# A list scheduler's cost figures set to other values, and PSUM evictions given another claim on buffers

## The chip, the cores and the metric

One NeuronCore of a Trainium2 chip. The metric is the device time of one execution in microseconds (us), the median of several runs. The time of one profiled execution stands beside it.

## The reference

Two layers of a decoder trunk with 512 tokens, 16 learned meta tokens ahead of them (528 columns) and a width of 2048. Everything is float32. Cut to what matters, one layer is:

```python
proj = h @ w_in                                   # 2048 -> 5120
c_val, c_glu, c_gate, q, k, v, a_gate, r_x, r_gate = split(proj)
c = depthwise_conv31(c_val * sigmoid(c_glu))
c = silu(layer_norm(c)) @ conv_pw_w + conv_pw_b
y_conv = c * silu(c_gate)
q, k = partial_rotary(q), partial_rotary(k)
y_attn = sliding_window_sink_attention(q, k, v) * silu(a_gate)
r = depthwise_conv4(r_x)
y_lru = rg_lru(r) * silu(r_gate)                  # a gated linear recurrence over positions
h = layer_norm(ALPHA * h + concat(y_conv, y_attn, y_lru) @ w_out)
```

A layer norm stands ahead of the first layer; the meta tokens are dropped from the output.

## The kernel before

Activations lie transposed: 128 channels on the partitions and the 528 tokens along a row, so the 2048 channels are 16 tiles. A float32 product is made of three float32r products (`mm3`): the rounded weight with the rounded activation, the rounded weight with the activation's remainder, and the weight's remainder with the rounded activation. Every weight block therefore comes by DMA into one of two raw buffers (`w`), ScalarE (ACT) rounds it and VectorE (DVE) subtracts to get the remainder (`weight_split`); the activations are split in the same way (`split`, and in `turn` and `normal` for the layers' inputs). The input projection of a layer has 40 column tiles, the output projection 16, each a sum over 16 row tiles. A full column tile is 96 products of 264 columns; where the second layer leaves the meta tokens out, a tile is 48 products of 512 columns.

No order is written out by hand. Each piece of work (`glu`, `val`, `rope`, `recur`, `gate`, `conv_taps`, `normal` and so on) is a generator that yields operations, allocations and conditions, a thread with a priority (a smaller number goes first). The class `Sched` runs these threads when the program is built: `run` looks at the head operation of each thread, works out when it could start (`_start`: when its engine is free by the costs booked so far, and when its operands are there by the hand-off times in `LAT`), and emits the operation with the earliest believed start; priority breaks ties. Each engine gets its instructions in the order in which they were emitted and carries them out in that order on the chip. So the booked costs decide nothing but the order. They are in `V` (DVE), `S` (ACT), `mm` and `tr` (TensorE, PE) and `dma` (the queue that SyncE issues).

Buffers come from pools: 78 activation rows (`u`), two PSUM tiles of two banks (`p`), four single banks (`b`), four temporaries (`t`), and others. An ordinary request for a `u` row is granted only while more than `10 - 2 * wheld` rows are free, `wheld` being the weight blocks split and not yet used up (`_head`); requests for split weights take the last row. A product's PSUM tile comes free after the thread that takes it has copied it out.

What the steps below touch: the statistics of the first two token tiles and their normalization (`x_norm`, `x_turn`, `turn`) with the first three column tiles (`gemms`); the end of layer 1 (`gather`, `square`, `norm`, `normal`), where the column sums of `norm` go through PE, a RECIPROCAL on DVE gives the scale of one half of the tokens, and each of 16 `normal` threads makes one tile of layer 2's input, the last step of which is a subtraction on DVE (the tile's remainder); and the recurrence (`recur`), of which at most two run at once and which has 12 products of its own.

Of the kernel before, what the change touches and what calls it, by code (L numbers as in the profile page):

```python
# [9 lines left out]
F32 = mybir.dt.float32  # L10
# [8 lines left out]
L = SEQ + NM  # L19
# [48 lines left out]
FULL = [(0, 0, HALF), (1, HALF, HALF)]  # L68
# [14 lines left out]


class Alloc:
    def __init__(self, kinds, dt=F32, w=L, weight=False):
        self.kinds, self.dt, self.w, self.weight = kinds, dt, w, weight


class Until:  # L90
# [4 lines left out]
class Sched:  # L95
# [5 lines left out]
    def __init__(self, tc, nc, pools):  # L101
        self.tc, self.nc, self.pools = tc, nc, pools
        self.free = dict.fromkeys("TVSGQ", 0.0)
        self.free["Q"] = 0.8
        self.fixed = ()
        self.threads = []
        self.written, self.read = {}, {}
        self.slots = {k: [(0.0, "Q", i) for i in range(n)] for k, (p, shape, n) in pools.items()}
        self.where = {}
        self.serial = 0  # L110
        self.wheld = self.steps = self.table = 0
# [65 lines left out]

    def mm(self, out, w, x, start, stop):
        n = self._size(x)
        c = max(n / 2400, self._size(w) / 1200) + 0.003  # L180
        if w.dtype == F32:
            c = 4 * c + 0.23
        f = self.nc.tensor.matmul
        return self._op("T", c, [out], [w, x], lambda: f(out, w, x, start=start, stop=stop))  # L184
# [5 lines left out]
    def dma(self, out, in_):  # L190
        f = self.nc.sync.dma_start
        n = 4 * self._size(out) * out.shape[0]
        o, i = ([a] if a.tensor.name in self.where or a.tensor.name in self.fixed else [] for a in (out, in_))
        return self._op("Q", max(0.45, n / 360e3), o, i, lambda: f(out=out, in_=in_), 2.0)  # L194


    def spawn(self, prio, gen):
# [12 lines left out]
    def _head(self, th):  # L210
        while True:
            r = th[3]
            if r is None or isinstance(r, Op):
                return r
            if isinstance(r, Event):
                if not r.done:
                    return None
                self._step(th, None)
            elif isinstance(r, Until):
                if not r.test():  # L220
                    return None
                self._step(th, None)
            else:
                kind = next((c for c in r.kinds if len(self.slots[c]) > (0 if r.weight or c != "u" else max(0, 10 - 2 * self.wheld))), None)
                if kind is None:
                    return None
                self._step(th, self.alloc(kind, r.dt, r.w))
# [45 lines left out]
def body(tc, nc, ctx, t):  # L273
# [85 lines left out]

    def U(dt=F32, w=L):  # L360
        return Alloc("u", dt, w)


    class Weight:
# [188 lines left out]
        pass  # L553

    def glu(y, j, pr):
        e = yield U()
        if j == 0:
            y.turn = yield Alloc("a")
        for pv, ev in pr.views(e):
            yield S(out=ev, in_=pv, func=AF.Tanh, scale=0.5)  # L560
        pr.free()
        y.glu[j] = e

    def val(y, j, pr):
        c = yield U()
        yield Until(lambda: y.glu[j] is not None)
        e = y.glu[j]
        for (pv, ev), (_, cv) in zip(pr.views(e), pr.views(c)):
            yield V("scalar_tensor_tensor", out=cv, in0=ev, scalar=1.0, in1=pv, op0=ALU.add, op1=ALU.mult)
        pr.free()  # L570
        k.release(e)
        k.spawn(6, conv_taps(y, j, c))
# [62 lines left out]
        k.release(y.turn)  # L635

    def conv_point(y, j, pr):
        o = yield U()
        for pv, ov in pr.views(o):
            yield S(out=ov, in_=pv, func=AF.Identity, scale=0.5, bias=P(y.l, "pb", j))  # L640
        pr.free()
        y.branch[8 + j] = o

    def rope(pr):
        a = pr.a
        x = yield U()
        s = yield U()
        for pv, xv in pr.views(x):
            yield S(out=xv, in_=pv, func=AF.Copy)
        pr.free()  # L650
        yield V("stream_shuffle", out=s[:, a:L], in_=x[:, a:L], mask=list(range(8, 16)) + list(range(8)) + list(range(16, 32)))
        yield V("tensor_tensor", out=x[:, a:L], in0=x[:, a:L], in1=cos[:, a:L], op=ALU.mult)
        yield V("tensor_tensor", out=s[:, a:L], in0=s[:, a:L], in1=sin[:, a:L], op=ALU.mult)
        yield V("tensor_tensor", out=x[:, a:L], in0=x[:, a:L], in1=s[:, a:L], op=ALU.add)
        k.release(s)
        return x
# [25 lines left out]
        k.release(x)  # L682

    def values(y, p, pr):
        x = yield U()
        m = yield U()
        for pv, xv in pr.views(x):
            yield S(out=xv, in_=pv, func=AF.Copy)
        pr.free()
        mv = m[:, 0:384].rearrange("p (n c) -> p n c", n=3)  # L690
        yield S(out=mv[:, :, 0:16], in_=x[:, 0:16].unsqueeze(1).to_broadcast([128, 3, 16]), func=AF.Copy)
        for i in range(3):
            yield S(out=mv[:, i, 16:128], in_=x[:, 88 + 100 * i:200 + 100 * i], func=AF.Copy)
        ps = []
        for _ in range(2):
            b = yield Alloc("b")
            ps.append(b)
        for n, pieces in enumerate(VCHUNKS):
            src = x[:, pieces[0][0]:pieces[0][0] + 128] if len(pieces) == 1 else mv[:, n // 2 - 1, :]
            yield k.tr(ps[n // 4][:, 128 * (n % 4):128 * (n % 4) + 128], src, ident)  # L700
        out = []
        for n in range(0, 8, 2):
            v = yield U(F32R, 512)
            v4 = v.rearrange("p (c g s d) -> p c g s d", c=2, g=2, s=2)
            p4 = ps[n // 4][:, 128 * (n % 4):128 * (n % 4) + 256].rearrange("p (c g d) -> p c g d", c=2, g=2)
            yield S(out=v4[:, :, :, 0, :], in_=p4, func=AF.Copy)
            yield V("tensor_tensor", out=v4[:, :, :, 1, :], in0=p4, in1=v4[:, :, :, 0, :].bitcast(F32), op=ALU.subtract)
            out.append(v)
        k.release(*ps, x, m)
        y.values[p] = out  # L710
# [107 lines left out]
            k.release(w)  # L818
            y.rw.append(p)

    def recur(y, j, pr):

        l, d = y.l, dp[y.l]
        x = yield U()
        for pv, xv in pr.views(x):
            yield S(out=xv, in_=pv, func=AF.Copy)
        pr.free()
        yield Until(lambda: y.busy < 2)
        y.busy += 1
        y.rgo = True  # L830
        r = yield U()
        yield S(out=r, in_=x, func=AF.Identity, scale=P(l, "lw", 12 + j), bias=P(l, "lb", j))
        for i in (2, 1, 0):
            s = 3 - i
# [32 lines left out]
    def gate(y, j, pr):  # L867

        a = pr.a
        e = yield U()  # L870
        for pv, ev in pr.views(e):
            yield S(out=ev, in_=pv, func=AF.Tanh, scale=0.5)
            yield V("scalar_tensor_tensor", out=ev, in0=ev, scalar=1.0, in1=pv, op0=ALU.add, op1=ALU.mult)
# [14 lines left out]
    def project(y, x, ready, phases):  # L888
# [12 lines left out]

        def step(fn, i, rngs, xs=x):
            pr = yield from gemm(xs, rngs)
            k.spawn(2 if fn is not recur else 7, fn(y, i, pr))

        k.spawn(0.2, recur_weights(y))
        todo = [(val, 1, FULL)][group - 3:]
# [1 line left out]
            todo += [(glu, j, FULL), (val, j, FULL)]  # L909
        todo += [(keys, 0, FULL), (values, 0, FULL)]  # L910
        todo += [(queries, j, rq) for j in range(4)]
        todo += [(recur, j, FULL) for j in range(4)]
        todo += [(keys, 1, FULL), (values, 1, FULL)]
        todo += [(gate, j, rq) for j in range(4)]
        todo += [(conv_point, j, rq, y.cx) for j in range(4)]
# [372 lines left out]
```

## Time and profile before

| | us |
|---|---|
| runs of the kernel | 1490.9, 1490.77, 1488.93 (median 1490.77) |
| the profiled execution | 1489.76 |
| its span | 1488.0 |
| PE busy in the span | 1451.8 (98%) |
| DVE busy | 1049.1 (71%) |
| ACT busy | 706.3 (47%) |

The mean granted clock of TensorE over the span was 0.995 of full speed. Times in rows are counted from the start of the span. A matmul's record is longer than the distance to the next one, since products are pipelined; so a stream of them is read by its starts or by a long row of the chain, and an idle time by the gap that a row names together with the lengths of the records around it.

### The profile page before, as it was taken

How to read it: one execution, taken by the hardware profiler on the slowest of the kernel's cores; microseconds unless marked ns; L12 is line 12 of the kernel's file. 1: busy time of each engine (PE TensorE's matmuls, PEld its weight loads, DVE VectorE, ACT ScalarE, POOL GpSimd, SP SyncE). 2: the span in 40 equal slices, each digit the busy share in tenths (PEclk: the TensorE clock that was granted, in tenths of full speed). 3: DMA queues.
4: the chain of work that ended last, by engine and by line, in shares of the span. 5: the costliest groups of instructions: out<-in, count | busy, mean ns of one | idle time of the engine just before them, and what ended most of it. 6: DMA issues, size and time to landing. Idle time of an engine off the chain costs nothing.

```text
span 1488.0 us, 25171 instructions
## 1 busy us (share of the span) xinstructions
PE 1451.8 (98%) x10028; PEld 1350.8 (91%) x10028; DVE 1049.1 (71%) x2111; ACT 706.3 (47%) x1539; POOL 20.3 (1%) x28
## 2 busy tenths in 40 slices
PE   4999999999999999999999999999999999999996
PEld 3999999999999999999999997998788888888885
DVE  7798999984588443354688889999747864434437
ACT  5412458883377332222368134778735853323221
POOL 2200000000000000000000000000000000000000
PEclk9999999999999999999999999999999999999999
DMA  6312522243221223232433033223232222523323
GB/s 231 93 57 85 143 86 65 62 138 106 80 72 58 85 86 114 72 100 85 132 111 93 29 107 120 79 61 118 88 103 86 71 72 90 163 88 114 100 71 113
DMA packets 56549, 142.32 MB, mean 96 GB/s; under 512 B 12464, under 2 KB 20912, under 8 KB 56432
## 3 DMA queue, kind: packets, MB, share of 16 engines
q1 hardware_dynamic: 56432, 140.73, 30.8%
q8 instruction: 78, 1.28, 0.4%
q14 instruction: 39, 0.32, 0.1%
HBM read 128.12 MB, written 4.19 MB: 89 GB/s over the span
## 4 chain that ended last, share of the span: by engine, by line
PE 88%; DVE 7%; ACT 2%; DMA 1%; issue 1%; SPq 0%; DVEq 0%; ACTq 0%
PE p L184 68%; PE b L184 18%; DVE u L160 5%; PE b L188 2%; DVE a L160 2%; ACT u L174 1%; DMA w<-in_win 1%; DVE s L160 0%; DMA a<-in_x 0%; DVE t L160 0%; ACT t L174 0%; DVE P L160 0%; DMA u<-u 0%; SPq L194 0%; PE p L188 0%
## 5 line engine op out<-in xcount | busy, mean ns | idle before, releaser
L184 PE MATMUL p<-u,u 128*128 128x264 f32 (+3 forms) x7824 | 1181.4, 306 | 4.1 <-DVE u L160 2.9
L184 PEld LDWEIGHTS p<-u,u 128*128 128x128 f32 x7824 | 1064.5, 189 | 61.8 <-DVE u L160 4.6
L160 DVE TENSOR_TENSOR u<-w,u 128x512 fp32r<-128x512 f32 x456 | 306.0, 689 | 174.0 <-ACT u L174 170.6
L174 ACT ACTIVATE u<-w 128x512 fp32r<-128x512 f32 x456 | 273.0, 622 | 241.8 <-DMA w<-in_wout 124.3
L184 PE MATMUL b<-u,u 128*128 128x512 f32 (+6 forms) x1568 | 290.5, 324 | 4.3 <-DVE u L160 3.2
L184 PEld LDWEIGHTS b<-u,u 128*128 128x128 f32 (+2 forms) x1568 | 241.4, 185 | 33.9 <-DVE u L160 4.6
L160 DVE SCALAR_TENSOR_TENSOR a<-u,dp,a 128x527 f32<-128x527 f32 (+14 forms) x240 | 179.7, 749 | 4.2
L174 ACT ACTIVATE P<-P,s 100x257 f32<-100x257 f32 (+5 forms) x240 | 111.2, 479 | 28.7 <-DVE s L160 28.7
L160 DVE TENSOR_TENSOR u<-u,u 128x528 f32<-128x528 f32 (+5 forms) x146 | 100.8, 697 | 20.8 <-ACT u L174 17.9
L174 ACT ACTIVATE u<-p 128x528 f32<-128x528 f32 (+2 forms) x71 | 42.4, 598 | 149.0 <-PE p L184 148.8
L174 ACT ACTIVATE u<-u 64x528 fp32r<-64x528 f32 (+5 forms) x112 | 63.8, 584 | 81.0 <-DVE u L160 74.9
L160 DVE SCALAR_TENSOR_TENSOR u<-u,p 128x528 f32<-128x528 f32 (+3 forms) x45 | 30.7, 683 | 68.7 <-ACT u L174 50.6
L174 ACT ACTIVATE t<-b 128x400 fp32r<-128x400 f32 (+3 forms) x112 | 57.1, 510 | 44.0 <-PE b L184 22.0
L160 DVE CUSTOM_DVE_ANT_0 P<-b,con,nsink 100x256 f32<-100x256 f32 (+2 forms) x160 | 67.1, 450 | 3.1 <-PE b L184 2.2
L160 DVE TENSOR_TENSOR t<-b,t 128x400 fp32r<-128x400 f32 (+2 forms) x72 | 41.7, 579 | 13.4 <-ACT t L174 13.0
L184 PE MATMUL b<-t,u 128*128 128x400 f32 (+2 forms) x144 | 50.5, 351 | 0.0
L188 PE MATMUL b<-con,P 100*128 100x100 f32 (+2 forms) x320 | 44.1, 253 | 0.0
L174 ACT ACTIVATE u<-b 128x256 fp32r<-128x256 f32 (+4 forms) x28 | 11.8, 443 | 57.7 <-PE b L188 51.1
L188 PEld LDWEIGHTS b<-con,P 100*128 100x128 f32 (+2 forms) x320 | 35.9, 140 | 3.1 <-DVE s L160 0.4
L160 DVE TENSOR_SCALAR P<-P,s 100x256 f32<-100x256 f32 (+3 forms) x88 | 31.5, 363 | 0.7
L160 DVE SCALAR_TENSOR_TENSOR u<-u,u 128x528 f32<-128x528 f32 (+1 forms) x40 | 27.5, 699 | 5.2 <-ACT u L174 4.7
L174 ACT ACTIVATION_READ_ACCUMULATOR P<-P,s 100x1 f32 (+2 forms) x160 | 30.2, 189 | 0.0
(103 smaller groups left out, 656.7 us busy)
## 6 DMA issues: line engine op xcount, KB each, us to landing
w<-in_win SPq DMA_DIRECT2D x160, 512.0 KB, 3.7
w<-in_wout SPq DMA_DIRECT2D x64, 512.0 KB, 4.1
u<-u SPq DMA_DIRECT2D x48, 120.0 KB, 2.2
a<-in_x SPq DMA_DIRECT2D x8, 256.0 KB, 5.1
P<-in_x SPq DMA_DIRECT2D x8, 256.0 KB, 6.0
u<-u SPq DMA_DIRECT2D x16, 128.0 KB, 2.1
w<-in_pw SPq DMA_DIRECT2D x8, 256.0 KB, 2.6
out<-a SPq DMA_DIRECT2D x8, 256.0 KB, 2.3
```

What stands on the lines that cost most here:

```text
L160: return self._op("V", c, outs, ins, lambda: f(**kw))
L174: op = self._op("S", c, outs, ins, lambda: f(**kw))
L184: return self._op("T", c, [out], [w, x], lambda: f(out, w, x, start=start, stop=stop))
L188: return self._op("T", max(2 * self._size(ident) / 2400, 0.11) + 0.005, [out], [x, ident], lambda: f(out, x, ident))
```

## The change

The booked durations change in three places. A product of n columns was booked at n/2400 us or the weight's columns/1200, whichever is more, and 0.003; it is now 0.000445 n or the same second term, and 0.0045. That is 0.113 before and 0.122 now for 264 columns, 0.216 and 0.232 for 512. A DMA was booked at its bytes/360,000 us and landed 2.0 later; now it is bytes/400,000 and 2.65, which for 512 KB is 3.46 before and 3.96 now. The queue is believed free from 0.75 on, before 0.8.

The row into which a PSUM tile is copied is now asked for with `E()`, which is granted while more than `4 - 2 * wheld` rows are free, in `glu`, `val`, `conv_point`, `rope`, `values` and `gate`. The second row of `rope` and `values` is asked for only after the PSUM tile has been given back. In the recurrence the copy out of PSUM becomes a thread of its own, `take_rx`, with `E()` and priority 2, which then starts `recur` at priority 7; before, the copy was the first step of `recur` and had priority 7.

```diff
-    def __init__(self, kinds, dt=F32, w=L, weight=False):
+    def __init__(self, kinds, dt=F32, w=L, weight=False, keep=10):
...
-        self.free["Q"] = 0.8
+        self.free["Q"] = 0.75
...
-        c = max(n / 2400, self._size(w) / 1200) + 0.003
+        c = max(0.445e-3 * n, self._size(w) / 1200) + 0.0045
...
-        return self._op("Q", max(0.45, n / 360e3), o, i, lambda: f(out=out, in_=in_), 2.0)
+        return self._op("Q", max(0.45, n / 400e3), o, i, lambda: f(out=out, in_=in_), 2.65)
...
-                kind = next((c for c in r.kinds if len(self.slots[c]) > (0 if r.weight or c != "u" else max(0, 10 - 2 * self.wheld))), None)
+                kind = next((c for c in r.kinds if len(self.slots[c]) > (0 if r.weight or c != "u" else max(0, r.keep - 2 * self.wheld))), None)
...
+    def E(keep=4):
+        return Alloc("u", F32, L, False, keep)
...
     def rope(pr):
         a = pr.a
-        x = yield U()
-        s = yield U()
+        x = yield E()
         for pv, xv in pr.views(x):
             yield S(out=xv, in_=pv, func=AF.Copy)
         pr.free()
+        s = yield U()
...
-    def recur(y, j, pr):
-
-        l, d = y.l, dp[y.l]
-        x = yield U()
+    def take_rx(y, j, pr):
+        x = yield E()
         for pv, xv in pr.views(x):
             yield S(out=xv, in_=pv, func=AF.Copy)
         pr.free()
+        k.spawn(7, recur(y, j, x))
+
+    def recur(y, j, x):
+
+        l, d = y.l, dp[y.l]
...
-            k.spawn(2 if fn is not recur else 7, fn(y, i, pr))
+            k.spawn(2, fn(y, i, pr))
...
-        todo += [(recur, j, FULL) for j in range(4)]
+        todo += [(take_rx, j, FULL) for j in range(4)]
```

The other five threads replace `U()` by `E()` in the same way. No operation is added or dropped: both programs have 10,022 matmuls and transposes on PE, 1,927 scheduled operations on DVE, 1,364 on ACT, 24 on GpSimd (POOL) and 395 DMAs. What changes is their order on each engine and the buffers that they get. In the pieces of that order below, a name is its pool, the count of the allocation and the tile's number; the last 200 operations of PE stand alike in both.

At the start, on DVE. `a_33` is the first token tile and `a_39` the second, BN_AGGR closes the statistics of the first. Before:

```order
L160 BN_STATS s_40_132<-a_33_121 128x6 x4
L160 BN_AGGR s_41_133<-s_40_132 128x2
L160 BN_STATS s_42_142<-a_39_131 128x6
L160 RECIPROCAL s_41_133<-s_41_133 128x1
L160 BN_STATS s_42_142<-a_39_131 128x6
L160 SCALAR_TENSOR_TENSOR s_41_133<-s_41_133 128x1
```

Now:

```order
L160 BN_STATS s_40_132<-a_33_121 128x6 x4
L160 BN_STATS s_42_140<-a_39_131 128x6
L160 BN_AGGR s_41_133<-s_40_132 128x2
L160 BN_STATS s_42_140<-a_39_131 128x6
L160 RECIPROCAL s_41_133<-s_41_133 128x1
L160 BN_STATS s_42_140<-a_39_131 128x6
L160 SCALAR_TENSOR_TENSOR s_41_133<-s_41_133 128x1
```

The first chunk of the second tile now has its statistics taken ahead of the first tile's BN_AGGR.

A little later on DVE, before the first weight of the third column tile gets its remainder (`u_86` before, `u_83` now, 128x512), which the third column tile's products on PE wait for. Before:

```order
L160 BN_STATS s_71_217<-P_57_185 128x6
L160 CAST u_15_101<-t_91_284 128x256
L160 TENSOR_SCALAR P_44_152<-P_44_152,s_52_177 128x512
L160 TENSOR_TENSOR u_16_102<-t_91_284,u_15_101 128x256
L160 CAST u_17_103<-t_93_294 128x256
L160 CAST u_19_105<-t_95_300 128x256
L160 TENSOR_SCALAR P_45_153<-P_45_153,s_52_177 128x512
L160 TENSOR_TENSOR u_86_263<-w_59_191,u_85_262 128x512
```

Now:

```order
L160 BN_STATS s_63_200<-P_54_177 128x6
L160 CAST u_13_99<-t_89_276 128x256
L160 TENSOR_SCALAR P_44_148<-P_44_148,s_52_173 128x512
L160 CAST u_15_101<-t_91_285 128x256
L160 CAST u_17_103<-t_93_292 128x256
L160 TENSOR_TENSOR u_16_102<-t_91_285,u_15_101 128x256
L160 TENSOR_TENSOR u_83_245<-w_65_204,u_82_244 128x512
```

The remainder stands ahead of one CAST and of the second normalized chunk (`P_45`), and one BN_STATS (of the fourth tile) has also gone behind it.

At the end of layer 1, on DVE. `a_1062` holds the scale of the tokens; its first write is a row of `norm` for the first half, which reads PSUM (`b`), and the 128x512 rows are remainders of weights. Before:

```order
L160 TENSOR_TENSOR a_1059_7223<-a_1059_7223,u_1258_9075 128x264
L160 TENSOR_TENSOR a_1059_7223<-a_1059_7223 128x264
L160 TENSOR_TENSOR u_1263_9112<-w_1252_9021,u_1262_9111 128x512
L160 TENSOR_TENSOR a_1062_7231<-b_1266_9128,a_1062_7231 128x264
L160 TENSOR_TENSOR u_1268_9137<-w_1257_9069,u_1267_9136 128x512
L160 TENSOR_TENSOR u_1270_9153<-w_1257_9069,u_1269_9152 128x512
L160 SCALAR_TENSOR_TENSOR u_1238_8930<-u_1238_8930,b_1259_9076 128x264
L160 TENSOR_TENSOR u_1238_8930<-u_1238_8930,a_1059_7223 128x264
L160 RECIPROCAL a_1062_7231<-a_1062_7231 128x264
```

Now:

```order
L160 TENSOR_TENSOR a_1059_7223<-a_1059_7223,u_1258_9076 128x264
L160 TENSOR_TENSOR u_1261_9095<-w_1252_9010,u_1260_9094 128x512
L160 TENSOR_TENSOR a_1059_7223<-a_1059_7223 128x264
L160 TENSOR_TENSOR a_1062_7231<-b_1263_9113,a_1062_7231 128x264
L160 TENSOR_TENSOR u_1265_9118<-w_1252_9010,u_1264_9117 128x512
L160 TENSOR_TENSOR u_1268_9137<-w_1257_9065,u_1267_9136 128x512
L160 RECIPROCAL a_1062_7231<-a_1062_7231 128x264
L160 TENSOR_TENSOR u_1270_9155<-w_1257_9065,u_1269_9154 128x512
```

The row of `norm` stands right behind the last addition of squares (`a_1059`), with no weight's remainder between, and its RECIPROCAL two places earlier. On PE the two products of `norm` stand ten places earlier.

The same place, some 45 rows on: the second half of the tokens. The rows that read a `t` write a remainder of layer 2's input, in the order of its tiles. Before:

```order
L160 TENSOR_TENSOR u_1313_9388<-t_1314_9389,u_1312_9387 128x264
L160 TENSOR_TENSOR P_1147_8096<-P_1147_8096,a_1062_7231 128x264
L160 TENSOR_TENSOR P_1159_8220<-P_1159_8220,a_1062_7231 128x264
L160 TENSOR_TENSOR u_1316_9393<-t_1317_9394,u_1315_9392 128x264
L160 RECIPROCAL a_1062_7231<-a_1062_7231 128x264
L160 TENSOR_TENSOR u_1319_9423<-t_1320_9424,u_1318_9422 128x264
L160 TENSOR_TENSOR a_1062_7231<-b_1307_9369,a_1062_7231 128x264
```

Now:

```order
L160 TENSOR_TENSOR u_1316_9398<-t_1317_9399,u_1315_9397 128x264
L160 TENSOR_TENSOR P_1159_8220<-P_1159_8220,a_1062_7231 128x264
L160 TENSOR_TENSOR u_1171_8344<-u_1171_8344,a_1062_7231 128x264
L160 TENSOR_TENSOR u_1319_9403<-t_1320_9404,u_1318_9402 128x264
L160 RECIPROCAL a_1062_7231<-a_1062_7231 128x264
L160 TENSOR_TENSOR u_1322_9431<-t_1323_9432,u_1321_9430 128x264
L160 TENSOR_TENSOR a_1062_7231<-b_1312_9381,a_1062_7231 128x264
```

The RECIPROCAL stands behind `u_1319`, which is tile 6 here, where before it stood behind `u_1316`, tile 5.

In layer 2, on PE, around the first gate tile (`p_1815` before, `p_1814` now; 128x512). The 128x264 products into `b` are those of the fourth recurrence. Before:

```order
L184 MATMUL p_1773_12588<-u_1345_9576,u_1766_12544 128x512
L184 MATMUL p_1773_12588<-u_1346_9577,u_1766_12544 128x512
L184 MATMUL p_1773_12588<-u_1345_9576,u_1767_12545 128x512
L184 MATMUL b_1813_12771<-u_1807_12751,u_1575_11447 128x264
L184 MATMUL b_1813_12771<-u_1808_12752,u_1575_11447 128x264
L184 MATMUL b_1813_12771<-u_1807_12751,u_1576_11448 128x264
L184 MATMUL p_1815_12781<-u_1286_9258,u_1769_12581 128x512
L184 MATMUL p_1815_12781<-u_1287_9259,u_1769_12581 128x512
L184 MATMUL p_1815_12781<-u_1286_9258,u_1770_12582 128x512
L184 MATMUL b_1816_12789<-u_1807_12751,u_1575_11447 128x264
L184 MATMUL b_1816_12789<-u_1808_12752,u_1575_11447 128x264
L184 MATMUL b_1816_12789<-u_1807_12751,u_1576_11448 128x264
```

Now:

```order
L184 MATMUL p_1814_12788<-u_1304_9345,u_1775_12616 128x512
L184 MATMUL p_1814_12788<-u_1305_9346,u_1775_12616 128x512
L184 MATMUL p_1814_12788<-u_1304_9345,u_1776_12617 128x512
L184 MATMUL p_1814_12788<-u_1307_9356,u_1782_12648 128x512
L184 MATMUL p_1814_12788<-u_1308_9357,u_1782_12648 128x512
L184 MATMUL p_1814_12788<-u_1307_9356,u_1783_12649 128x512
L184 MATMUL p_1814_12788<-u_1315_9397,u_1782_12648 128x512
L184 MATMUL p_1814_12788<-u_1316_9398,u_1782_12648 128x512
L184 MATMUL p_1814_12788<-u_1315_9397,u_1783_12649 128x512
L184 MATMUL b_1818_12822<-u_1807_12762,u_1575_11449 128x264
L184 MATMUL p_1814_12788<-u_1318_9402,u_1782_12648 128x512
```

Before, all twelve products of the recurrence stood among the first products of this gate tile, the first three of them ahead of it; now eighteen of the gate's products stand ahead of the first of the recurrence's, and they are spread out behind.

## Rows read from the trace of the kernel before

**Rows 1.** The page: busy time by engine, and the chain's shares.

```profile
PE 1451.8 (98%) x10028; PEld 1350.8 (91%) x10028; DVE 1049.1 (71%) x2111; ACT 706.3 (47%) x1539; POOL 20.3 (1%) x28
...
PE 88%; DVE 7%; ACT 2%; DMA 1%; issue 1%; SPq 0%; DVEq 0%; ACTq 0%
```

**Rows 2.** Stretches: length, busy per engine (x instructions), granted clock, DMA share, GB/s.

```profile
20.00:30.00 10.00, 6.97 (x31) 4.84 (x30) 10.00 (x22) 6.34 (x14) 6.83 (x8) 0.85 0.23 71
30.00:40.00 10.00, 10.00 (x73) 10.00 (x72) 9.14 (x22) 4.70 (x9) 2.84 (x3) 0.81 0.72 226
40.00:1477.00 1437.00, 1431.21 (x9918) 1333.72 (x9917) 1010.08 (x2027) 683.90 (x1498) 9.73 (x12) 1.00 0.30 92
80.00:160.00 80.00, 80.00 (x661) 80.00 (x660) 72.83 (x118) 19.16 (x35) 0.00 (x0) 1.00 0.25 75
740.00:800.00 60.00, 58.86 (x470) 57.76 (x469) 54.53 (x132) 43.99 (x85) 0.00 (x0) 1.00 0.28 83
800.00:900.00 100.00, 100.00 (x770) 97.30 (x770) 85.31 (x133) 33.87 (x63) 0.00 (x0) 1.00 0.32 97
900.00:1050.00 150.00, 147.03 (x1024) 136.30 (x1023) 143.19 (x316) 108.53 (x263) 0.00 (x0) 1.00 0.29 90
```

**Rows 3.** The chain that ended last: start, length, what (x instructions).

```profile
489.55 239.90 PE p L184 x1966
...
1214.24 77.73 PE p L184 x336
```

**Rows 4.** Timeline of the start: start, length, engine, instruction [idle before <-what ended it].

```profile
6.95 0.26 DVE L160 BATCH_NORM_AGGREGATE s<-s 128x2 f32<-128x24 f32 x1
...
8.73 0.69 DVE L160 BATCH_NORM_STATS2 s<-a 128x6 f32<-128x512 f32 x1 [1.51 <-DMA a<-in_x]
...
10.17 1.52 ACT L174 ACTIVATE a<-a,s 128x512 f32<-128x512 f32 x2 [2.62 <-DVE s L160]
...
25.81 0.48 DVE L160 CAST u<-t 128x256 fp32r<-128x256 f32 x2
...
26.21 0.97 DVE L160 TENSOR_SCALAR P<-P,s 128x512 f32<-128x512 f32 x1
...
27.10 1.21 DVE L160 TENSOR_TENSOR u<-w,u 128x512 fp32r<-128x512 f32 x1
...
28.37 0.58 PE L184 MATMUL b<-u,u 128*128 128x256 f32 x1 [2.04 <-DVE u L160]
```

**Rows 5.** Timeline at the end of layer 1, DVE and PE.

```profile
774.06 1.80 DVE L160 RECIPROCAL a<-a 128x264 f32<-128x264 f32 x1 [0.40 <-ACT a L174]
...
775.78 0.37 DVE L160 TENSOR_TENSOR u<-t,u 128x264 fp32r<-128x264 f32 x1
...
777.64 0.28 PE L184 MATMUL p<-u,u 128*128 128x264 f32 x1
...
778.12 0.42 DVE L160 TENSOR_TENSOR u<-t,u 128x264 fp32r<-128x264 f32 x1
...
778.60 0.88 PE L184 MATMUL p<-u,u 128*128 128x264 f32 x5 [0.68 <-DVE u L160]
```

**Rows 6.** Timeline, four late starts of PE elsewhere.

```profile
75.33 0.75 PE L184 MATMUL p<-u,u 128*128 128x264 f32 x4 [0.21 <-ACT u L174]
...
290.85 0.63 PE L184 MATMUL p<-u,onesr 128*128 128x264 f32 x3 [0.64 <-DVE u L160]
...
1028.64 1.43 PE L184 MATMUL p<-u,u 128*128 128x512 f32 x5 [0.70 <-ACT u L174]
...
1045.67 0.50 PE L184 MATMUL p<-u,u 128*128 128x512 f32 x1 [0.69 <-DVE u L160]
```

**Rows 7.** The page's DMA groups (KB, us to landing); a group of DVE (busy, mean).

```profile
w<-in_win SPq DMA_DIRECT2D x160, 512.0 KB, 3.7
...
w<-in_wout SPq DMA_DIRECT2D x64, 512.0 KB, 4.1
...
L160 DVE TENSOR_TENSOR_SCAN u<-u,u 128x528 f32<-128x528 f32 x8 | 9.9, 1246 | 0.0
```

More of the change, by code (lines that the diff above doesn't have):

```diff
@@ L85 @@
 class Alloc:
-    def __init__(self, kinds, dt=F32, w=L, weight=False):
-        self.kinds, self.dt, self.w, self.weight = kinds, dt, w, weight
+    def __init__(self, kinds, dt=F32, w=L, weight=False, keep=10):
+        self.kinds, self.dt, self.w, self.weight, self.keep = kinds, dt, w, weight, keep
 class Until:
@@ L555, in glu @@
     def glu(y, j, pr):
-        e = yield U()
+        e = yield E()
         if j == 0:
@@ L564, in val @@
     def val(y, j, pr):
-        c = yield U()
+        c = yield E()
         yield Until(lambda: y.glu[j] is not None)
@@ L637, in conv_point @@
     def conv_point(y, j, pr):
-        o = yield U()
+        o = yield E()
         for pv, ov in pr.views(o):
@@ L684, in values @@
     def values(y, p, pr):
-        x = yield U()
-        m = yield U()
+        x = yield E()
         for pv, xv in pr.views(x):
@@ L689, in values @@
         pr.free()
+        m = yield U()
         mv = m[:, 0:384].rearrange("p (n c) -> p n c", n=3)
@@ L819, in recur_weights @@
             y.rw.append(p)
-    def recur(y, j, pr):
-        l, d = y.l, dp[y.l]
-        x = yield U()
+    def take_rx(y, j, pr):
+        x = yield E()
         for pv, xv in pr.views(x):
@@ L869, in gate @@
         a = pr.a
-        e = yield U()
+        e = yield E()
         for pv, ev in pr.views(e):
```

## The prediction, made before the changed kernel ran

> **What bounds the kernel now.** Read the page's busy times first, then the chain, then PE's idle time by stretches. PE works 1451.8 of 1488 us, and the chain that ended last lies on it for 88% [rows 1]. Neither number tells what PE's pace is; the chain's long rows do. 1966 products of 264 columns take 239.90 us, so 122.0 ns each, and 336 of 512 columns take 77.73, so 231.3 ns each [rows 3]. No operand is late there. This work is the same after the change, product for product, so some 1,450 us can't move; only PE's late starts can, and the start and the tail, which are fixed by other engines.
>
> How much are the late starts? From 40 to 1477 us PE is busy 1431.21 of 1437, so it shows 5.8 us of idle time [rows 2]. That is too little: the record of one 264-column product is 0.28 us long [rows 5], 0.16 more than the pace, so each late start hides another 0.16. The timeline has 16 of them, the first at 75.33 and the last at 1045.67 [rows 6]; 16 times 0.16 is 2.6, and the whole is 8.4 us. By place: the end of layer 1 (740 to 800) 1.14 idle and six starts, 2.1; layer 2's attention and recurrence (900 to 1050) 2.97 and five, 3.8 [rows 2]; the other five 1.7 and 0.8, so 2.5. Their releasers are mostly DVE. [...]
>
> **The change, part by part.** None of it alters an operation, so the price of each edit is what the new order does at those places.
>
> *The booked product.* 0.113 and 0.216 become 0.122 and 0.232, which is what rows 3 measure. With the old figures the scheduler believed PE 7% faster than it is; it put PE's next products, and the work that feeds them, ahead of whatever DVE could have done meanwhile. With the new ones DVE is believed to have more room and takes more of the convolution's taps before the same product of PE: some 8 to 15 more by the time the scores of either layer begin. The room is there: DVE works 72.83 of 80 us in 80 to 160 and 85.31 of 100 in 800 to 900, while PE doesn't idle in either [rows 2]. Each tap that moves forward leaves later DVE time free where DVE is nearly full, 143.19 of 150 in 900 to 1050 [rows 2]. That is the gain's main source.
>
> [...]
>
> *The booked DMA.* For 512 KB the landing moves from 3.46 to 3.96 us; the medians are 3.7 and 4.1 [rows 7]. It only moves requests earlier or work on a weight later. Weights are split some 90 products (11 us) ahead of PE in both orders, and PE's late starts name ACT or DVE, not a DMA [rows 6]: taken at nothing in the steady part. At the start it moves a row: below.
>
> *Evictions with `E()`, and `take_rx`.* A copy out of PSUM may now take a row when more than 4 are free, and the recurrence's copy no longer has the lowest claim. PE waited at 1028.64 for such a copy, 0.70 idle and 0.16 hidden [rows 6]. If rows run out elsewhere instead, an ordinary request waits; cover for that is DVE's and ACT's idle time, and without it the price is one late start, 0.4 to 0.9 each as in rows 6.
>
> *The start.* The first tile's BN_AGGR now stands behind a statistic that waits for its DMA until 8.73; it ran at 6.95 [rows 4]. So it ends at about 9.7 instead of 7.2, and the first normalization on ACT begins at about 11.1 instead of 10.17 [rows 4]. DVE does not lose all of this: 1.51 us it waited for that DMA anyway, and it has other statistics to do; it loses the 0.26 of BN_AGGR, which no longer fills the wait, and some 0.2 behind the root on ACT, 0.5 in all. Against that, the remainder of the third weight has less ahead of it: a statistic (0.69), a normalized chunk (0.97) and a CAST (0.24) [rows 4], 1.9 us. DVE has no gap there, so the remainder ends 1.4 earlier than 28.31 (27.10 and 1.21), and PE, which took it up at 28.37 [rows 4], goes on at about 27.0. I take 1.3 off. Bounds: if PE is soon short of normalized inputs, which are moved back by the same rows, nothing is kept and the 0.9 of the later first normalization is lost; if the clock comes back earlier too, up to 2.5 is won.
>
> *The end of layer 1.* The row of `norm` stands ahead of a weight's remainder (some 0.7, as the 128x512 row in rows 4 at 8.73) and its products ten places earlier on PE (1.2 us), so the scale of both halves is there about 1.2 earlier. PE's last late start there is tile 7's remainder: it came behind a RECIPROCAL of 1.80 and tile 6's, and PE started at 778.60 instead of 777.76 (777.64 and the pace), 0.84 late [rows 5], on top of a smaller lateness for tile 6. With the RECIPROCAL one tile later, tile 6's goes; with everything 1.2 earlier most of tile 7's is covered too. Of 2.1 I leave 0.6: minus 1.5.
>
> *Layer 2, 900 to 1050.* The two starts at 1044 and 1045.67 come from a recurrence whose products stand in fours with single gate products, so that a DVE remainder is waited for with nothing else to do. With eighteen gate products (4.2 us by rows 3) ahead, both have cover. The copy at 1028.64 is moved up by its claim. Of 3.8 I leave 1.3: minus 2.5.
>
> *The other five.* The scores' first product and the means of the convolution's norm (290.85, 0.64 idle [rows 6]) are chains of DVE and ACT that taps moved forward shorten but don't remove: of 2.5 I leave 1.5, minus 1.0.
>
> *New waits.* In the new order an operand's last step stands five to seven products ahead of its use, 0.6 to 0.85 us, and one subtraction of 264 columns takes 0.42 [rows 5] besides hand-offs: it holds, but thinly. For eight new late starts of 0.16 I add 1.3.
>
> Sum: -1.3 - 1.5 - 2.5 - 1.0 + 1.3 = -5.0. Against the profiled execution's 1489.76 that is 1484.8. That execution lies 1.0 under the runs' median of 1490.77, so for the median I say **1485.8**.
>
> **The rivals.**
> *The waits only move (no difference).* PE's work is fixed, and DVE's too; with a truer table the scheduler spends the cover that the false one left by mistake. If each wait that goes comes back as another of like size, 3 to 4 us of the 6.3 won are lost, and the time is 1488 to 1491. For it: the thin lead above. Against: the places that wait now are where DVE is full, and taps do go out of them.
> *DVE is over-filled (slower).* The old table's 7% made PE really arrive later than believed, a cover for everything DVE is booked too cheaply for. The recurrence's scan is booked at 0.615 (its 528 columns and 62, by 960 MHz) and takes 1.246 [rows 7]; eight of them are 5.0 us short, and they lie where DVE is at 143.19 of 150. If the taps that fill 60 to 180 and 800 to 900 also stand ahead of remainders that PE now reaches on time, PE waits for the 5.0, none of the old 6.3 in layers goes, and the time is 1490.8 + 5.0 - 1.3 = 1494.5. It decides from the point at which DVE has no gap left before a remainder: 85.31 of 100 and some ten taps more (7 to 8 us) is 93, under it. So it is less likely than the forecast.
> *More is won.* All 8.4 us go and the start gives 2.5: 1479.9. It needs the scores' and means' chains to vanish, which no moved row does.
> *The order doesn't do what the change says.* The moved rows stand in the order as told, so only their effect is open; no chance of its own.
>
> **How the numbers follow.** A measurement of this kernel can tell about 0.2%, 3.0 us, from no change: faster is under 1487.8, slower over 1493.8. The forecast (most waits go, 1482 to 1487.8) has 0.56; more is won (under 1482) 0.08; the waits only move (1487.8 to 1493.8) 0.25; over-filled DVE, or the start's loss together with it, 0.11. So faster 0.64, same 0.25, slower 0.11. The range leaves out most of the greater gain (0.06), the slower case (0.11) and the upper end of the middle one (0.03): 1481.5 to 1491.5.
>
> **What would show it right or wrong.** Right: PE goes on at about 27.0 at the start; the stretch around the end of layer 1 has under 0.5 of visible idle time and the attention and recurrence of layer 2 under 1.2; DVE is over 90 of 100 busy in 800 to 900; the pace of the long rows stays at 122 and 231 ns. Wrong: PE resumes after 28.4 or the granted clock stays low past 34; new gaps in 60 to 160 or 800 to 900 released by DVE, which is the over-filled case; or gaps released by ACT, where a row (`u`) was missing.

## The result: 20 us slower, and the profile after

The changed kernel takes 1510.23 us (1507.62 to 1511.55) where the kernel before, run beside it, takes 1490.03. The ratio is 1.0132 with an interval of 1.0117 to 1.0147. I had said 1485.8, within 1481.5 to 1491.5; the sign is wrong and the size is beyond any of my cases. The profiled execution of the changed kernel (called after from here on) took 1511.55, 1.3 more than the median of its runs; its span is 1509.7.

The page of after, the lines that answer to [rows 1]:

```profile
PE 1466.9 (97%) x10028; PEld 1354.9 (90%) x10028; DVE 1052.1 (70%) x2111; ACT 705.8 (47%) x1539; POOL 21.0 (1%) x28
...
PE 76%; DVE 15%; ACT 4%; DMA 3%; issue 2%; SPq 0%; DVEq 0%; ACTq 0%
```

PE has 76% of the chain instead of 88: DVE has 15 instead of 7, ACT 4 instead of 2, DMA 3 instead of 1. PE is "busy" 15 us longer with the same 10028 instructions. The chain's long rows show that its pace is what it was, 122.1 and 231.3 ns [rows 3]:

```profile
497.44 234.86 PE p L184 x1924
...
1230.62 83.02 PE p L184 x359
```

By stretches, shifted to where the same work now lies (columns as in [rows 2]):

```profile
30.00:40.00 10.00, 9.96 (x77) 9.76 (x77) 9.18 (x21) 4.08 (x8) 2.71 (x4) 1.00 0.64 213
40.00:1498.00 1458.00, 1444.38 (x9909) 1336.40 (x9909) 1013.24 (x2027) 683.55 (x1498) 9.84 (x12) 1.00 0.30 91
80.00:160.00 80.00, 80.00 (x660) 80.00 (x659) 75.82 (x117) 17.12 (x29) 0.00 (x0) 1.00 0.23 68
755.00:815.00 60.00, 59.33 (x477) 58.41 (x477) 55.65 (x135) 44.73 (x87) 0.00 (x0) 1.00 0.30 83
815.00:915.00 100.00, 99.06 (x759) 96.13 (x759) 89.67 (x138) 32.85 (x61) 0.00 (x0) 1.00 0.33 97
915.00:1070.00 155.00, 150.13 (x1018) 136.42 (x1016) 146.35 (x319) 111.42 (x267) 0.00 (x0) 1.00 0.29 87
```

Visible idle time from 40 us on is 13.6 us, before 5.8 [rows 2]; that explains 8 of the 21.7 us by which the span grew. The rest hides in PE's busy time. The stretch 200 to 280, first of before, then of after, shows it: 80.00 of 80 us busy becomes 78.22, but 660 instructions become 617.

```profile
200.00:280.00 80.00, 80.00 (x660) 79.53 (x659) 75.97 (x199) 63.48 (x178) 0.00 (x0) 1.00 0.23 69
```
```profile
200.00:280.00 80.00, 78.22 (x617) 75.36 (x616) 74.90 (x199) 63.47 (x179) 0.00 (x0) 1.00 0.22 66
```

So I compared starts: when PE begins its n-th instruction in after, less the same for before (us; the same for four of the experiments below, "best" being the last kernel under "Both covers"). Each column is one execution.

| PE instruction | after | product only | all but product | truer DVE, ACT | best |
|---|---|---|---|---|---|
| 360 | -1.0 | +0.1 | -1.1 | -2.5 | -0.8 |
| 1000 | +2.1 | -0.0 | -1.1 | -1.8 | -0.8 |
| 1300 | +5.3 | +3.3 | -1.5 | -1.0 | -1.5 |
| 2400 | +12.4 | +11.4 | +0.3 | +2.5 | -1.7 |
| 3500 | +14.4 | +13.4 | +0.1 | +2.6 | -1.9 |
| 6000 | +15.0 | +13.5 | -0.1 | +3.1 | -1.8 |
| 6100 | +12.9 | +13.4 | +0.6 | +1.1 | -1.8 |
| 7000 | +14.7 | +13.5 | +1.7 | +3.1 | -1.8 |
| 7900 | +20.6 | +21.4 | +2.8 | +6.5 | -2.8 |
| 10000 | +21.8 | +24.6 | +1.8 | +4.1 | -3.8 |

In after, some 10 us go between instructions 1000 and 2400, layer 1's attention and recurrence (154 to 337 us), and 7 between 7000 and 8900, the same in layer 2. The start won 1 us and the end of layer 1 won 2, as I had said.

The place where it begins is the first product of layer 1's scores. On DVE, and PE's wait, in after:

```profile
177.28 0.70 DVE L160 TENSOR_TENSOR u<-u,u 128x528 f32<-128x528 f32 x1
177.90 1.56 DVE L160 SCALAR_TENSOR_TENSOR a<-u,dp,a 128x525 f32<-128x525 f32 x2
179.49 0.70 DVE L160 TENSOR_TENSOR u<-u,u 64x528 fp32r<-64x528 f32 x1
180.22 0.69 DVE L160 TENSOR_TENSOR u<-w,u 128x512 fp32r<-128x512 f32 x1
180.93 0.70 DVE L160 TENSOR_TENSOR u<-u,u 64x528 fp32r<-64x528 f32 x1
...
180.25 0.44 PE L184 MATMUL b<-u,u 128*128 128x128 f32 x2 [1.46 <-DVE u L160]
```

The query's last rope step (177.28) is followed by two taps of the convolution (`a<-u,dp,a`, 1.56 us), then by its remainder (179.49), and PE has waited for it. DVE has no gap here. Before, the same rows stood there, two taps included, and PE's wait was 0.48:

```profile
174.79 1.51 DVE L160 SCALAR_TENSOR_TENSOR a<-u,dp,a 128x504 f32<-128x504 f32 x2
...
176.94 0.70 DVE L160 TENSOR_TENSOR u<-u,u 64x528 fp32r<-64x528 f32 x1
...
177.74 0.41 PE L184 MATMUL b<-u,u 128*128 128x128 f32 x2 [0.48 <-ACT u L174]
```

The scores' remainder is DVE's 312th scheduled step in after and its 304th before. Eight steps more, at some 0.7 us, are 5.6 us of work; in the plan they fitted. What they cost can't be read from 179.49 against 176.94, since some 3 us of after's time at this point come from one late transfer at 75.89 (under "Which booking"). The experiment with the scan's booking alone has the same order up to 290 us and not that transfer; its rows here, and DVE's work up to the remainder, of before and then of that run:

```profile
175.23 0.70 DVE L162 TENSOR_TENSOR u<-u,u 64x528 fp32r<-64x528 f32 x1
...
175.99 0.44 PE L186 MATMUL b<-u,u 128*128 128x128 f32 x2 [1.45 <-DVE u L162]
```
```profile
0.00:176.94 176.94, 157.31 (x1204) 150.44 (x1205) 152.37 (x310) 67.91 (x129) 20.34 (x28) 0.98 0.40 124
```
```profile
0.00:175.23 175.23, 155.38 (x1200) 148.01 (x1200) 158.89 (x318) 67.36 (x127) 21.18 (x28) 1.00 0.40 125
```

DVE's idle time ahead of the remainder falls from 24.6 to 16.3 us: the eight steps go into it, and the remainder even comes 1.7 us earlier than before. But PE comes earlier still. It is 2.2 us ahead by instruction 1000, the scores stand five products further forward in its order, and it starts its last product ahead of them 2.7 us earlier than before (174.25 against 176.98). So its wait grows by 1 us.

### The profile page after: what moved, and what is told of

It reads as the page before. It is cut to its first block, busy times and chain, and to the rows that moved or that the text cites. A ratio compares the mean times of both kernels' runs of the same rounds, so it can differ in the third digit from the quotient of the medians.

```text
span 1509.7 us, 25187 instructions
## 1 busy us (share of the span) xinstructions
PE 1466.9 (97%) x10028; PEld 1354.9 (90%) x10028; DVE 1052.1 (70%) x2111; ACT 705.8 (47%) x1539; POOL 21.0 (1%) x28
## 4 chain that ended last, share of the span: by engine, by line
PE 76%; DVE 15%; ACT 4%; DMA 3%; issue 2%; SPq 0%; DVEq 0%; ACTq 0%
PE p L184 59%; PE b L184 15%; DVE u L160 9%; DVE a L160 3%; ACT u L174 3%; PE b L188 2%; DMA w<-in_win 2%; DVE P L160 1%; DMA w<-in_wout 1%; DVE s L160 1%; DMA a<-in_x 0%; SPq L194 0%; ACT t L174 0%; ACT a L174 0%; DMA u<-u 0%
## 5 line engine op out<-in xcount | busy, mean ns | idle before, releaser
L184 PE MATMUL b<-u,u 128*128 128x512 f32 (+6 forms) x1568 | 296.2, 327 | 7.6 <-DVE u L160 5.7
L184 PE MATMUL b<-t,u 128*128 128x400 f32 (+2 forms) x144 | 53.7, 373 | 0.5 <-DVE t L160 0.3
L160 DVE TENSOR_TENSOR t<-b,t 128x400 fp32r<-128x400 f32 (+2 forms) x72 | 41.6, 578 | 14.7 <-ACT t L174 14.4
L184 PEld LDWEIGHTS b<-t,u 128*128 128x128 f32 x144 | 27.0, 188 | 6.2 <-ACT t L174 1.7
```

The lines of the kernel that those rows point to most:

```text
L160: return self._op("V", c, outs, ins, lambda: f(**kw))
```

## The experiments

**Which edit.** Four kernels, each with a part of the change. The product alone:

```diff
-        c = max(n / 2400, self._size(w) / 1200) + 0.003
+        c = max(0.445e-3 * n, self._size(w) / 1200) + 0.0045
```

> The kernel before with one edit: the booked duration of a product set to the measured one. Theory 'lost cover': with the old figure PE really arrived at each place later than the scheduler believed, and that hid everything DVE, ACT and the DMAs are booked too cheaply for; with the measured figure each such error makes PE wait. Then this edit alone makes most of the 20 us: 1503 to 1513, with new late starts of PE where the convolution's taps fill DVE (150 to 330 and 900 to 1060 us). Rival 'rows and queue': the loss comes from the eviction claims or from the booked DMA, which put the rounding of weights and other rows ahead of copies out of PSUM on ACT; then this edit alone gives 1484 to 1494.

Measured 1514.44 us, ratio 1.0159 (1.0143 to 1.0174). The whole loss, and more.

The booked DMA alone:

```diff
-        return self._op("Q", max(0.45, n / 360e3), o, i, lambda: f(out=out, in_=in_), 2.0)
+        return self._op("Q", max(0.45, n / 400e3), o, i, lambda: f(out=out, in_=in_), 2.65)
```

> The kernel before with one edit: the booked DMA (512 KB landing at 3.96 instead of 3.46 us, queue free from 0.75). 'Lost cover': a longer booked transfer is nearer to the measured 3.7 to 4.1 and takes no cover from PE: 1486 to 1494. Rival 'queue': the later believed landing moves weights' rounding in front of the copies out of PSUM: 1498 or more.

Measured 1496.67, ratio 1.0042 (1.0027 to 1.0056): between the two expectations. 5.6 us of it are lost between instructions 1800 and 2200 (250 to 300 us), where the booked DMA makes a different order on DVE and PE:

```profile
250.00:300.00 50.00, 46.85 (x355) 45.50 (x355) 43.28 (x87) 39.75 (x87) 0.00 (x0) 0.93 0.18 54
```

PE idles for 3.2 us there, and the granted clock is 0.93, where before has 1.00 in the same stretch, so that part of the loss seems to be clock. Beside the eviction claims this loss is not there (next but one), so it seems to belong to that order and not to the booking as such; which operation is late first was not taken apart.

The eviction claims alone:

```diff
-        x = yield U()
+        x = yield E()
...
+        k.spawn(7, recur(y, j, x))
```

> The kernel before with one edit: the eviction claims (E with 4 rows kept, rope's and values' second row later, take_rx at priority 2). 'Lost cover': 1484 to 1493, copies out of PSUM are no later than before. Rival 'rows': rows run short and other work waits: 1498 or more.

Measured 1489.53, ratio 0.9993 (0.9983 to 1.0002): no difference.

The change without the product:

```diff
-        c = max(0.445e-3 * n, self._size(w) / 1200) + 0.0045
+        c = max(n / 2400, self._size(w) / 1200) + 0.003
```

> The changed kernel with the old booked product (n/2400 and 0.003), everything else as changed. 'Lost cover': the loss goes, 1484 to 1494, and the late starts of PE in 150 to 330 fall from some 12 us to under 3. Rivals 'rows' and 'queue': it keeps most of the loss, 1500 or more.

Measured 1491.79, ratio 1.0010 (1.0000 to 1.0019). The loss is gone. So the booked product makes it, alone (1514.44) or with the rest; rows, priorities and the queue by themselves don't.

**Why a truer figure costs 20 us.** The scheduler's own believed times, which building the program gives, stand beside the measured ones (us, start of the n-th PE instruction):

| instruction | before: believed, measured, behind | after | truer DVE, ACT |
|---|---|---|---|
| 1000 | 133.7, 152.3, 18.6 | 140.4, 154.4, 14.0 | 140.4, 150.5, 10.1 |
| 2400 | 294.7, 324.7, 30.0 | 314.6, 337.1, 22.5 | 313.7, 327.2, 13.5 |
| 7000 | 824.4, 890.9, 66.5 | 882.6, 905.6, 23.0 | 881.7, 894.0, 12.4 |
| 8900 | 1136.7, 1223.3, 86.6 | 1214.1, 1245.0, 30.9 | 1214.2, 1227.2, 13.0 |
| last | 1374.1, 1476.4, 102.3 | 1468.5, 1498.2, 29.7 | 1468.5, 1480.5, 12.0 |

Before, PE falls behind its plan all the way, 102 us in all, because each product takes 7 to 8% longer than booked. DVE and ACT then have that much more time for everything. After, PE keeps its plan's pace in the even stretches (22.5 and 23.0 at 2400 and 7000) and falls behind only in the attention and recurrence: 8.5 us and 7.9 us. There DVE and ACT have steps that are booked too cheaply, and now nothing makes up for it; that this is why is what the next experiment tests. The rows for it: DVE's steps on 64 partitions take 0.73 from start to start (179.49 to 180.22 above) and are booked at 0.615, which is (528 + 62)/960 in `V` and which the 128-partition step at 177.28 does take (0.62). The shuffle takes 0.79 (start to the next start, 172.33 below, in before), booked at 0.615. The scan is 1.25 [rows 7] and 1.17 from start to start (288.94 to 290.11 in before). The subtractions of `values` wait in turn for ACT's copy out of the same PSUM tile and come at 0.87 and 0.34, booked at 0.33 (last two rows below, in after). ACT's roundings on 64 partitions last 0.644 in the mean of 32 and are booked at 0.529.

```profile
171.54 0.75 DVE L160 STREAM_SHUFFLE u<-u 128x528 f32<-128x528 f32 x1
172.33 1.33 DVE L160 TENSOR_TENSOR u<-u,con 128x528 f32<-128x528 f32 x2
```
```profile
905.33 0.42 DVE L160 TENSOR_TENSOR u<-b,u 128x256 fp32r<-128x256 f32 x1
906.20 0.76 DVE L160 TENSOR_TENSOR u<-b,u 128x256 fp32r<-128x256 f32 x2 [0.45 <-ACT u L174]
```

All of these set right on the changed kernel:

```diff
+        if name == "tensor_tensor_scan":
+            c += 0.55
+        elif name == "stream_shuffle":
+            c += 0.175
+        elif outs[0].shape[0] == 64:
+            c += 0.12
+        elif ps and len(outs[0].shape) > 3:
+            c += 0.27
...
+        if outs[0].shape[0] == 64:
+            c += 0.13
         f = self.nc.scalar.activation
```

> The changed kernel with the DVE and ACT steps that the trace shows longer than booked set to what it shows: the scan +0.55 us, the shuffle of rope +0.175, steps that write 64 partitions +0.12 on DVE and +0.13 on ACT, the four subtractions of values +0.27. Theory 'lost cover by DVE's bookings': these are what the true product duration laid bare in the attention and recurrence, so 8 to 14 of the 20 us come back: 1496 to 1502. Rival 'thin leads': the greedy order puts each operand only just ahead of its use whatever is booked, and any delay costs; then these bookings change little: 1506 to 1513.

Measured 1493.56, ratio 1.0022 (1.0012 to 1.0032): 16.7 of the 20.2 us come back, more than I expected. PE's falling behind between 2400 and 8900 is gone from the table (13.5, 12.4, 13.0); between 1000 and 2400 3.4 us of 8.5 are left. What the last 3.5 us are was not taken apart. Its idle time from 40 us on, and the stretch that had 617 instructions:

```profile
40.00:1481.00 1441.00, 1434.01 (x9897) 1332.71 (x9896) 1011.92 (x2025) 681.06 (x1496) 9.84 (x12) 1.00 0.30 92
```
```profile
197.00:277.00 80.00, 79.16 (x637) 77.49 (x636) 76.20 (x200) 65.23 (x181) 0.00 (x0) 1.00 0.21 64
```

7.0 us of idle time instead of 13.6, 637 instructions instead of 617 in 80 us. The expectation's rival, that any thin lead costs whatever is booked, is out by this.

**The rival on the DMA.** In after's profile PE starts a product at 75.89 that has waited 1.73 us for a copy out of PSUM; on ACT two roundings of weights stand ahead of that copy, and they waited for a transfer of 5.63 us, where 3.96 is booked.

```profile
68.48 5.63 DMA w<-in_win
...
74.14 1.15 ACT L174 ACTIVATE u<-w 128x512 fp32r<-128x512 f32 x2 [2.25 <-DMA w<-in_win]
...
75.89 1.35 PE L184 MATMUL p<-u,u 128*128 128x264 f32 x6 [1.73 <-ACT u L174]
```

```diff
-        return self._op("Q", max(0.45, n / 400e3), o, i, lambda: f(out=out, in_=in_), 2.65)
+        return self._op("Q", max(0.45, n / 400e3), o, i, lambda: f(out=out, in_=in_), 4.3)
```

> The changed kernel with the DMA's landing booked 1.65 us later (512 KB at 5.6 us, the slowest one seen ahead of a late start). If the roundings of weights that wait for a DMA in front of copies out of PSUM are a main part, the late starts of PE at 75.9 and 829.8 go and 4 to 6 us come back: 1504 to 1507. If DVE's bookings are the main part, what remains is 1503 to 1512, with the late starts in 150 to 330 and 900 to 1060 unchanged.

Measured 1511.92, ratio 1.0147 (1.0130 to 1.0163): nothing comes back. The start at 75.9 is on time, but between PE's instructions 100 and 360 the longer booking loses 3.6 us instead.

Both edits, the truer bookings and the later DMA:

```diff
+            c += 0.55
...
+        return self._op("Q", max(0.45, n / 400e3), o, i, lambda: f(out=out, in_=in_), 4.3)
```

> Both of the last two edits on the changed kernel. 'Lost cover' with these two as the whole of it: 1488 to 1497, the sum of the two. 'Thin leads': 1503 or more.

Measured 1494.57, ratio 1.0029 (1.0017 to 1.0040): as with the DVE and ACT bookings alone. The DMA is no main part. It may have a small one: this kernel, too, loses 3.7 us between instructions 100 and 360, but behind instruction 1000 only 2.6, where the truer DVE and ACT bookings alone lose 5.9 (one execution each).

**How much cover.**

```diff
-        c = max(0.445e-3 * n, self._size(w) / 1200) + 0.0045
+        c = max(0.428e-3 * n, self._size(w) / 1200) + 0.0045
```

> The changed kernel with a product of 264 columns booked at 0.1175, half way between old and new (512: 0.2236). 'Lost cover': PE still arrives some 4% later than believed, about 50 us by the end, and each stretch of 100 products then forgives 0.45 us of underbooking; most of the loss goes, 1491 to 1500, nearer the old end. If instead a particular order that 0.122 happens to give were to blame, there is no reason for a point between: 1489 to 1493 or 1505 to 1513.

Measured 1497.99, ratio 1.0055 (1.0039 to 1.0071): half the cover forgives 12 of the 20 us. It is a matter of degree and not of one unlucky order.

**Which booking.** The scan alone, on the changed kernel:

```diff
+        if name == "tensor_tensor_scan":
+            c += 0.55
```

> The changed kernel with only the scan's booking raised by 0.55 us. The scans come at the end of each layer's recurrence, behind most of the lost time of 150 to 290 us, and two of the eight lie where PE waits for DVE at all; if each error is paid only where it stands, 1 to 4 us come back, all of them behind 290 and behind 1000: 1505 to 1510. If the scan (the one row that the prediction named) is the main part, as eight times 0.55 and what follows from it: 1495 to 1502.

Measured 1508.93, ratio 1.0124 (1.0110 to 1.0138). That is 1.3 us, no more than the intervals of the two kernels leave open (after: 1.0117 to 1.0147): the row that my prediction named for this rival is by itself worth little or nothing. This kernel has the same order as after up to 290 us, and there its copy is not late; PE runs through:

```profile
73.11 3.07 PE L186 MATMUL p<-u,u 128*128 128x264 f32 x23
```

So the 3 us that after's profiled execution loses at 75.89 (+3.1 from instruction 360 to 400) come from a slow transfer in that execution, and the order by itself doesn't bring them. How often such a transfer comes isn't shown; after's four executions lie 3.9 us apart. The start's gain varies as well: with the same order it is 2.0 us at instruction 360 here and 1.0 in after.

The steps on 64 partitions and the shuffle alone (and the 0.13 on ACT):

```diff
+        if name == "stream_shuffle":
+            c += 0.175
+        elif outs[0].shape[0] == 64:
+            c += 0.12
```

> The changed kernel with only the bookings of steps that write 64 partitions (+0.12 on DVE, +0.13 on ACT) and of the shuffle (+0.175) raised. These belong to the making of keys and queries and to the end of the mix, which lie among the taps in 150 to 290: if errors are paid where they stand, most comes back: 1496 to 1502. If the scan is the main part: 1504 to 1510.

Measured 1503.17, ratio 1.0086 (1.0070 to 1.0101): 7.1 us, between the two expectations.

The subtractions of `values` alone:

```diff
+        if name == "tensor_tensor" and ps and len(outs[0].shape) > 3:
+            c += 0.27
```

> The changed kernel with only the booking of the subtractions of values raised (+0.27 us, sixteen in the kernel). Scan alone gave back 1.3 us and the half-partition steps with the shuffle 7.1, of 16.7 for all. If the rest is this edit's by itself: 1500 to 1504. If it is that the bookings only help together, as any one that is left puts PE behind DVE again: 1506 to 1511.

Measured 1508.93, ratio 1.0124 (1.0106 to 1.0143): 1.3 us, again within the intervals.

All but `values`, the truer bookings less one branch:

```diff
-        elif ps and len(outs[0].shape) > 3:
-            c += 0.27
```

> The truer bookings without those of values (scan, half-partition steps, shuffle). If values has 8 us of its own: 1500 to 1503. If the bookings help mainly together with the scan: 1494 to 1498.

Measured 1496.61, ratio 1.0047 (1.0032 to 1.0062): 13.6 us, where the scan and the others give 1.3 and 7.1 by themselves. So the bookings seem to help together: 1.3 + 7.1 + 1.3 = 9.7 one by one, 16.7 all at once. Each of these differences is known to some 2 to 3 us, so the surplus of 7 is likely and not certain. I read it so that any one that is left still lets DVE fall behind later in the same stretch; that is not shown, and which one is paid where wasn't taken apart.

**Both covers.** The truer bookings with the old product:

```diff
-        c = max(0.445e-3 * n, self._size(w) / 1200) + 0.0045
+        c = max(n / 2400, self._size(w) / 1200) + 0.003
```

> The changed kernel with the truer DVE and ACT bookings of e5 and the old, too short booking of a product. If a booking that believes PE too fast is a cover against whatever is still booked too cheaply, this has both and is the fastest so far: 1483 to 1490, with the start's gain of 1 us kept. If the truer bookings alone do the work and cover is of no use beside them, it is like e5: 1491 to 1495.

Measured 1488.91, ratio 0.9992 (0.9983 to 1.0000): some 4.5 us under the truer bookings with the true product, and no different from before.

And with the old DMA besides:

```diff
-        return self._op("Q", max(0.45, n / 400e3), o, i, lambda: f(out=out, in_=in_), 2.65)
+        return self._op("Q", max(0.45, n / 360e3), o, i, lambda: f(out=out, in_=in_), 2.0)
```

> As the last one, with the old booked DMA too, so that only the eviction claims and the truer DVE and ACT bookings differ from the kernel before. The booked DMA cost 6 us alone and 2 us beside the eviction claims; without it this should be 0 to 3 us under the last one: 1482 to 1489. The rival (cover of no use): 1490 to 1495.

Measured 1486.31, ratio 0.9973 (0.9964 to 0.9983): the one kernel that is clearly faster than the kernel before, by 4.0 us. With the eviction claims alone the ratio was 0.9993, so the truer DVE and ACT bookings gain some 3 us beside the old product too. From 40 us on:

```profile
40.00:1473.00 1433.00, 1429.36 (x9911) 1333.21 (x9909) 1011.70 (x2027) 690.62 (x1502) 9.74 (x12) 1.00 0.30 92
```

3.6 us of idle time. It keeps the false product, the old DMA, and takes from the change only the eviction claims. In the table of starts it is the only column that loses in neither layer.

## Why the prediction was wrong, step by step

*Pace and fixed work.* Right: 122.1 and 231.3 ns.

*The start, -1.3.* Right: PE is 1.3 us ahead by instruction 100 and 1.0 by 360 (2.0 in the other traced execution of this order, above). PE takes up the third column tile's remainder at 27.17 (I said 27.0), and the clock stays at 1.00 from 30 to 40, where before it was 0.81:

```profile
25.89 1.22 DVE L160 TENSOR_TENSOR u<-w,u 128x512 fp32r<-128x512 f32 x1
...
27.17 0.58 PE L184 MATMUL b<-u,u 128*128 128x256 f32 x1 [0.25 <-DVE u L160]
```

*The end of layer 1, -1.5.* (The row at 8.73 that I took for the length of a weight's remainder is a statistic's; the remainder's mean on the page is 0.689, so the size holds.) Right for the place and not for what was left of it: 2.1 us are won between instructions 6000 and 6100, and 1.8 of them go again by 6400, with a late start at 793.64 for a later tile's remainder and one at 829.79 for a copy out of PSUM:

```profile
793.64 0.64 PE L184 MATMUL p<-u,u 128*128 128x264 f32 x3 [0.44 <-DVE u L160]
...
829.79 0.99 PE L184 MATMUL p<-u,u 128*128 128x264 f32 x6 [0.94 <-ACT u L174]
```

*The booked product, "the gain's main source".* This is the step that failed. I saw that the new figure is the measured one, that DVE takes eight and more steps in front of the scores, and that DVE had idle time before them; and I concluded that these steps go into that idle time and free DVE later. They do go into it, but PE's wait at the scores grows by 1 us all the same, and DVE isn't free later: in layer 2's attention and recurrence it works 146.35 of 155 us, and PE idles for 4.87 there where it idled for 2.97 of 150. What I left out is what the old error did: with PE 8% slower than believed, every other booking had 8% of slack, and the change takes that away for all of them at once. *Layer 2, -2.5*, became +7.0; *the other five, -1.0*, became some +10 in layer 1; *new waits, +1.3*, was the term that should have held it all.

*The rival "DVE is over-filled".* Its mechanism is what happened, and I gave it 0.11. Two of its terms were mis-sized. Its price, 5.0 us, was the scan's eight errors, and the scan is worth 1.3, within the intervals; the steps on 64 partitions, the shuffle and `values` stood in the same trace and I hadn't set their starts against their bookings. And the point from which it decides, "DVE has no gap left", was read in 800 to 900 (85.31 of 100) and not where the taps are followed by the scores: 143.19 of 150 in 900 to 1050 [rows 2] was the row, with taps ahead of steps that PE waits for.

*The signs that I had set.* Pace and start came as said. The others failed: the end of layer 1 has 0.67 us of idle time in its 60 us (I had said under 0.5), layer 2's attention and recurrence 4.87 (under 1.2), and DVE works 89.67 of 100 where I had said over 90. The sign of the over-filled case was set at the wrong places as well, gaps in 60 to 160 and 800 to 900 that DVE ends: the two gaps there, at 75.89 and 829.79, were ended by ACT, and those that DVE ends begin with the scores at 180.

*What hid it from me.* To count late starts, with 0.16 hidden in each, was the right way to read idle time, though the trace of before has 13 with idle time from 40 us on and not 16, which takes 0.5 off the 8.4. But I priced new ones as eight more of the least size; after has 28, and seven of them idle for 0.8 us or more. Set against the usual step of each shape, starts from 40 us on that are late by 0.2 us or more sum to 18.4 us in after (7.8 before), and those late by 0.02 to 0.2 to 24.7 (13.5): half of the new loss is in delays too short to be seen as idle time. By estimate some 3 us of them lie in the two stretches with a granted clock of 0.57 (next section but one).

## What to carry to other kernels

A list scheduler's durations are a set: an engine booked too fast gives every other booking slack, and putting that one figure right shows all other errors at once. Measure each engine's steps, start to start, against their bookings before correcting the one that bounds the kernel, or leave it a few per cent short on purpose: here half the error was worth 12 us, and the fastest kernel had the whole error and truer DVE and ACT bookings. And where filler work is ordered among steps that the bounding engine waits for, ask at those steps whether the filling engine has any gap, not in the stretch ahead.

## What the runs showed of the hardware

After two of the late starts the granted clock fell: it was 0.57 over 4 us each, behind idle times of 1.73 and of 1.46 and 0.39 us. The second is in the scan-only run too, at the same place and behind a wait of 1.45 (last row):

```profile
76.00:80.00 4.00, 4.00 (x21) 4.00 (x22) 3.90 (x16) 1.75 (x4) 0.00 (x0) 0.57 0.47 136
182.00:186.00 4.00, 4.00 (x22) 4.00 (x22) 3.96 (x12) 2.25 (x7) 0.00 (x0) 0.57 0.02 4
```
```profile
178.00:182.00 4.00, 4.00 (x23) 4.00 (x22) 3.96 (x12) 2.33 (x7) 0.00 (x0) 0.57 0.04 6
```

Each such stretch holds 21 to 23 instructions where 33 of 122 ns would fit, by this estimate some 1.3 us lost on top of the wait. Other waits, as the 0.94 us at 829.79, had no such follow-up (granted clock 1.00 from 830 to 834). These late starts thus cost more than their waits, in busy time that looks like work.
